# Four pairs of the second feed-forward as block products, with weight sums made ahead of it

## The chip, the cores and the metric

The kernel runs on one core of one Trainium2 chip. The metric is the device time of one execution in microseconds, the median of several runs. One core has five engines that work side by side: TensorE (PE, matrix products), VectorE (DVE), ScalarE (ACT), GpSimd (POOL) and SyncE (SP), and 16 DMA engines that move data between the chip's memory (DRAM) and the core's. Each engine works off its own instructions in order; waits between engines go by semaphores.

## The reference

One residual block for 256 tokens of width 1024: a feed-forward, a mix of two attention-like branches, a memory read, and a second feed-forward.

```python
def swiglu(h, w_in, w_down):
    gate, up = jnp.split(h @ w_in, 2, axis=-1)
    return (jax.nn.silu(gate) * up) @ w_down
...
        h = rmsnorm(x, ffn1_pre_g[l])
        x = x + 0.5 * rmsnorm(swiglu(h, ffn1_w_in[l], ffn1_w_down[l]), ffn1_post_g[l])

        h = rmsnorm(x, mix_pre_g[l])
        q_a, f_a, i_a, g_a, q_b, k_b, v_b, f_b, gates = jnp.split(h @ w_in[l], IN_OFFSETS, axis=-1)
        ...   # HGRN2 recurrence -> y_a, forgetting attention -> y_b, gated sum y
        x = x + rmsnorm(y @ w_out[l], mix_post_g[l])

        h = rmsnorm(x, mem_pre_g[l])
        mem_n = rmsnorm(mem, mem_kv_g[l])
        x = x + rmsnorm(mem_cross_attention(h, mem_n, w_mq[l], w_mkv[l], w_mo[l]), mem_post_g[l])

        h = rmsnorm(x, ffn2_pre_g[l])
        x = x + 0.5 * rmsnorm(swiglu(h, ffn2_w_in[l], ffn2_w_down[l]), ffn2_post_g[l])
```

The width of the feed-forward's inside (D_FF) is 2816. All inputs and outputs are float32.

## The kernel before

**Products.** Every operand is kept as two float32r parts, hi (rounded) and lo (the rest), and each product is made as three: hi·hi, hi·lo, lo·hi. Weights come as units of 128x1024 float32 (512 KB). `load_split` loads a unit on SP's queue into one of four `raw` buffers; ACT copies it to `hi` (L129), VectorE subtracts to make `lo` (L130); hi and lo have eight buffers each. The order of the units is that in which the code calls for them, and they are loaded and split that far ahead as the buffers allow. TensorE's order is the order in which its instructions are written, save for blocks that `after(i)` puts behind the i-th matmul of the log.

**Stages in time.** First feed-forward (to about 188 us of the span), the mix (projections i_a, f_a, q_a, g_a; HGRN2; q_b, k_b, v_b and the forgetting attention; gates; br_a, br_b; w_out), the memory read (mk, mv, mq, mo), the second feed-forward (from about 601 us), and a tail: the last norm, done by `post_last`, and the output.

**A feed-forward** goes over NFF = 11 chunks of 256 columns of gate and 256 of up. A plain chunk takes four units: for each half of the tokens (128), 8 blocks of 128 rows x 3 products of 512 columns go into a bank of PSUM; `act_evac` makes silu(gate)·up from it, `flush` turns that on TensorE (L386) and splits it, and `down` multiplies it with two units of the down weights, 24 products of 512 columns per chunk, into four accumulators that stay open over all chunks.

**Pairs as block products.** For a pair of chunks (c, c+1) named in QUADS_1 or QUADS_2, `quad` treats two token halves, two halves of the inner dimension and the two chunks as a 2x2 block product and makes it with seven products in place of eight (a scheme of Strassen's kind): 7 x 4 blocks x 3 = 84 products of 512 columns. It needs sums of activations (made once by `mixed`, with the splits and the row scale in it; this is `mix[0]`, the activations N) and sums of weight blocks. The sums of weights are made inside of `quad`: four units are loaded plain (to `raw`), four to two `wide` buffers, VectorE adds them (L446 to L449, and L503 in place), and `two` splits the sums as if they were loaded. `fourth_product` and `third_product` end the quad. In the last quad of a feed-forward that ends with it (`last`, c = 9) their order is the other way round. Both feed-forwards have quads at chunks 5 and 8, so that chunks 0 to 4, 7 and 10 are plain.

**The tail's warm-up.** In the second feed-forward, when the second half of chunk 10 has been evacuated, `act_evac` issues one Sqrt on a single column (L408); `post_last` needs a Sqrt at its end (L348).

**GpSimd** does little: the moves of the attention's cumulated logarithms through DRAM (`cd`, `cbc`, `cbm`, L885 to L935) with DMAs on its own queue, and two selects (L937).

The `wide` buffers hold the first heads, the weights of a quad, and in the mix the gates' bias rows (`brow`).

Of the kernel before, what the change touches and what calls it, by code (L numbers as in the profile page):

```python
# [49 lines left out]

QUADS_1 = (5, 8)
QUADS_2 = (5, 8)
# [18 lines left out]
def block_kernel(ctx: ExitStack, tc: tile.TileContext, wts, head_in, gf_in, x_in, mem_in, memT_in, cols, rows, fbias, masks, out):  # L71
# [194 lines left out]
    def mixed(X, r):  # L266

        row = row_of(r)
# [102 lines left out]
    def ffn(w_in, w_dn, X, r2, n_tok, i_row, quads, first_half, second_half=None):  # L371
# [46 lines left out]
        def quad(c, n_down):  # L418
# [10 lines left out]
            B11, B21, wide, first, second_, fourth = ([] for _ in range(6))  # L429
            for q in range(2):  # L430
                W = wp.tile([P, 2, 2, 512], F32, tag="wide", name=nm("wide"), bufs=2)
                raws = []
                for i in range(2):
                    u = _AT[w_in] + 4 * c + 2 * q + i
                    raw = wp.tile([P, D], F32, tag="raw", name=nm("raw"), bufs=4)
                    loads.append(nc.sync.dma_start(raw, wts[u - 4]).ins)
                    loads.append(nc.sync.dma_start(W[:, i].rearrange("p j n -> p (j n)"), wts[u]).ins)
                    hi, lo = parts_of()
                    split(hi, lo, raw)
                    B11.append((hi[:, :512], lo[:, :512]))  # L440
                    B21.append((hi[:, 512:], lo[:, 512:]))
                    raws.append(raw)
                wide.append(W)
                t1, t2, t4 = (m4([P, 2, 512], n="sum") for _ in range(3))
                for i in range(2):
                    V.tensor_tensor(out=t1[:, i], in0=raws[i][:, :512], in1=W[:, i, 0], op=ALU.add)  # L446
                V.tensor_tensor(out=t2, in0=t1, in1=W[:, :, 1], op=ALU.add)
                for i in range(2):
                    summed = V.tensor_tensor(out=t4[:, i], in0=t2[:, i], in1=raws[i][:, 512:], op=ALU.add).ins  # L449
                first.append(t1)  # L450
                second_.append(t2)
                fourth.append(t4)
            T1 = two(first[0]) + two(first[1])
# [29 lines left out]
            if len(late) == 2:  # L483
                flush(n + 4)
                flush(n + L_ACT)
            else:
                with tc.issue_after(summed):
                    flush(n + L_ACT)
# [5 lines left out]
            T2 = two(second_[0]) + two(second_[1])  # L494
            prods(b1, F(s2h, s2l), T2, False)
# [5 lines left out]
            T3 = []  # L501
            for W in wide:
                V.tensor_tensor(out=W[:, :, 0], in0=W[:, :, 0], in1=W[:, :, 1], op=ALU.add)  # L503
                T3 += two(W[:, :, 0])
# [7 lines left out]
            def fourth_product():  # L512
                T4 = two(fourth[0]) + two(fourth[1])
                prods(b1, X(1, 1), T4, False, True)
                act_evac(b1, c, 1)

            def third_product():
                B22 = two(wide[0][:, :, 1]) + two(wide[1][:, :, 1])
                prods(b2, F(s4h, s4l), B22, False, True)
                V.tensor_tensor(out=w, in0=b2, in1=w, op=ALU.subtract)  # L520
                act_evac(w, c + 1, 0)

            if last:
                down(n_down + 1, 1)
                flush_half(c + 1, 1, n + L_ACT)
                third_product()
                n = len(log)
                fourth_product()
                flush_half(c + 1, 0, n + 12)
            else:  # L530
                fourth_product()
                down(n_down + 1, 1)
                third_product()
# [47 lines left out]
        for c in range(n_tok, NFF):  # L581
# [6 lines left out]
            acts[c] = m4([P, 2, 2, T], F32R, "act")  # L588
            if c == 2 and first_half:
# [105 lines left out]

    ffn("f1_in", "f1_dn", X1, norm_1, 0, 0, QUADS_1, first)


    iv = [m4([P, 2, 512], n="iv") for _ in range(2)]
    for h in range(2):  # L700
# [5 lines left out]
        if h == 0:  # L706
            half(X2, r2, 1, G_MIX, m + L_IA)
    row2 = row_of(r2)
# [19 lines left out]
    for c in range(2):  # L728
# [12 lines left out]
        kT_.append(k)  # L741
    for c in range(2):
# [9 lines left out]
        qT_.append(q)  # L752

# [135 lines left out]
    for c in range(2):  # L889
        for name, lst, sc in (("k_b", kb_, 1.0), ("q_b", qb_, 1.0 / math.sqrt(128.0))):  # L890
# [7 lines left out]
            lst.append(t)  # L898
            if c == 0 and name == "k_b":
# [109 lines left out]
    for c in range(2):  # L1009
# [6 lines left out]
        vb_.append(t)  # L1016
    for h in range(2):
# [5 lines left out]
    brows = []  # L1023

    def gates(c):
        u = chunk("gates", c)
        z = m4([P, 2, 512], n="zg")
        if c % 2 == 0:
            brows.append(wp.tile([P, 2, D], F32, tag="wide", name=nm("brow"), bufs=2))
        brow = brows[-1][:, c % 2, :512]  # L1030
# [6 lines left out]
        zs.append(z)  # L1037

    m = len(log)
    gates(0)  # L1040
    for g in range(2):
# [20 lines left out]
    for c in (0, 2, 1, 3):  # L1062
        S.activation(zs[c], zs[c], AF.Sigmoid)
    g2 = load_row(1)
# [11 lines left out]
    for c in range(2):  # L1076
        for name, X, zc in (("br_a", OA, c), ("br_b", OB, 2 + c)):
            u = chunk(name, c)
            for h in range(2):
# [9 lines left out]
                if zc != c:  # L1089
                    za = zs[c][:, h]  # L1090
                    V.tensor_tensor(out=za, in0=za, in1=z, op=ALU.add)

# [13 lines left out]
    for h in range(2):  # L1106
        rows_proj(po[h], Y, "w_out", h, range(0, 4))
        if h == 0:
            y_T(1, 1, m + L_Y)
    rowm = row_of(rm)  # L1110
# [9 lines left out]
    for c in range(2):  # L1120
        u = chunk("mk", c)
        KM.more()
        for j in range(2):
# [4 lines left out]
            split(KM.h[c][:, js], KM.l[c][:, js], t)  # L1128
            if j == 0:
                half(X3, r3, c, G_MEM, m + (L_WO, L_MK)[c], m + (L_WO, L_MK)[c] + 16)  # L1130
    for c in range(2):
        u = chunk("mq", c)
        QM.more()
        for j in range(2):
            js = slice(2 * j, 2 * j + 2)
            ps = proj_col2(X3, u, (2 * j, 2 * j + 1))
            split(QM.h[c][:, js], QM.l[c][:, js], ps)

# [55 lines left out]

    m = len(log)
    mem_v(1)
    for i in range(2):
# [22 lines left out]
    ffn("f2_in", "f2_dn", X4, r4, 2, 3, QUADS_2, None, second)  # L1220
# [85 lines left out]
```

## Time and profile before

| | |
|---|---|
| median of 3 runs | 790.78 us (790.71 to 791.66) |
| the profiled execution's own time | 791.19 us |
| its span | 789.3 us |
| granted TensorE clock, mean | 0.999 |
| PE / DVE / ACT / POOL busy | 779.5 / 609.5 / 451.5 / 9.3 us |
| moved by DMA | 147.44 MB, mean 187 GB/s |

The span runs from the first instruction's start to the last end in the profile; the execution's own time has about 1.9 us around it. Busy time counts the work of an engine without its waits. TensorE's ends are modelled, so what counts for it is the time from start to start.

### The profile page before, as it was taken

How to read it: one execution, taken by the hardware profiler on the slowest of the kernel's cores; microseconds unless marked ns; L12 is line 12 of the kernel's file. 1: busy time of each engine (PE TensorE's matmuls, PEld its weight loads, DVE VectorE, ACT ScalarE, POOL GpSimd, SP SyncE). 2: the span in 40 equal slices, each digit the busy share in tenths (PEclk: the TensorE clock that was granted, in tenths of full speed). 3: DMA queues.
4: the chain of work that ended last, by engine and by line, in shares of the span. 5: the costliest groups of instructions: out<-in, count | busy, mean ns of one | idle time of the engine just before them, and what ended most of it. 6: DMA issues, size and time to landing. Idle time of an engine off the chain costs nothing.

```text
span 789.3 us, 12909 instructions
## 1 busy us (share of the span) xinstructions
PE 779.5 (99%) x5028; PEld 674.5 (85%) x5028; DVE 609.5 (77%) x944; ACT 451.5 (57%) x682; POOL 9.3 (1%) x21
## 2 busy tenths in 40 slices
PE   9999999999999999999999999999999999999996
PEld 7878888888899999998888888999888888888885
DVE  6798989978766898578685665965758799978963
ACT  7655665656853447348584444754636665664751
POOL 0000000000000100100000000000000000000000
PEclk9999999999999999999999999999999999999999
DMA  9766483384544555644497655456454545471441
GB/s 340 244 246 228 157 298 136 135 285 161 169 153 143 181 188 164 232 156 137 150 327 272 220 171 176 162 170 203 151 170 133 194 153 209 152 275 71 147 161 53
DMA packets 43692, 147.44 MB, mean 187 GB/s; under 512 B 4840, under 2 KB 8304, under 8 KB 43632
## 3 DMA queue, kind: packets, MB, share of 16 engines
q1 hardware_dynamic: 43024, 144.92, 53.7%
q0 software_dynamic: 464, 1.58, 0.6%
q8 instruction: 39, 0.64, 0.3%
q14 instruction: 21, 0.17, 0.1%
q10 hardware_dynamic: 144, 0.13, 0.0%
HBM read 145.56 MB, written 1.06 MB: 186 GB/s over the span
## 4 chain that ended last, share of the span: by engine, by line
PE 95%; DMA 2%; ACT 1%; DVE 1%; issue 0%; DVEq 0%; SPq 0%; ACTq 0%
PE mm L85 64%; PE acc L85 27%; PE tr L85 3%; DMA raw<-in_wts_dram 1%; PE tr L386 1%; PE tr L306 1%; DMA head<-in_head_dram 1%; ACT hi L129 0%; DVE lo L130 0%; PE tr L983 0%; PE tr L1072 0%; PE tr L1175 0%; ACT hT L148 0%; DVEq L1302 0%; SPq L655 0%
## 5 line engine op out<-in xcount | busy, mean ns | idle before, releaser
L130 DVE TENSOR_TENSOR lo<-raw,hi 128x1024 fp32r<-128x1024 f32 (+1 forms) x228 | 271.6, 1207 | 68.4 <-ACT hi L129 64.1
L129 ACT CAST hi<-raw 128x1024 fp32r<-128x1024 f32 (+1 forms) x228 | 232.2, 1036 | 127.0 <-PE mm L85 76.7
L85 PE MATMUL mm<-hi,hT 128*128 128x512 f32 (+1 forms) x496 | 189.7, 385 | 0.9 <-ACT hT L148 0.9
L85 PE MATMUL mm<-lo,hT 128*128 128x512 f32 (+1 forms) x496 | 190.2, 386 | 0.0
L85 PE MATMUL mm<-hi,lT 128*128 128x512 f32 (+1 forms) x496 | 188.5, 385 | 0.0
L85 PE MATMUL acc<-hi,act 128*128 128x512 f32 x352 | 113.2, 391 | 0.0
L85 PEld LDWEIGHTS mm<-hi,hT 128*128 128x128 f32 x496 | 93.1, 188 | 19.5 <-ACT hT L148 1.6
L85 PE MATMUL mm<-hT,hi 128*128 128x256 f32 x384 | 109.0, 284 | 0.1
L85 PE MATMUL mm<-hT,lo 128*128 128x256 f32 x384 | 109.0, 284 | 0.0
L85 PE MATMUL mm<-lT,hi 128*128 128x256 f32 x384 | 108.9, 284 | 0.0
L85 PEld LDWEIGHTS mm<-hi,lT 128*128 128x128 f32 x496 | 93.1, 188 | 17.7 <-DVE lT L264 0.7
L85 PEld LDWEIGHTS mm<-lo,hT 128*128 128x128 f32 x496 | 93.0, 188 | 16.5
L85 PEld LDWEIGHTS acc<-hi,act 128*128 128x128 f32 x352 | 66.0, 188 | 14.0 <-DVE act L149 0.5
L85 PEld LDWEIGHTS mm<-hT,hi 128*128 128x128 f32 x384 | 73.6, 192 | 0.4 <-issue 0.3
L85 PEld LDWEIGHTS mm<-lT,hi 128*128 128x128 f32 x384 | 73.6, 192 | 0.1
L85 PEld LDWEIGHTS mm<-hT,lo 128*128 128x128 f32 x384 | 73.6, 192 | 0.1
L85 PE MATMUL acc<-lo,act 128*128 128x512 f32 x176 | 69.2, 393 | 0.0
L85 PEld LDWEIGHTS acc<-lo,act 128*128 128x128 f32 x176 | 33.1, 188 | 6.6
L85 PE MATMUL acc<-hi,hT 128*128 128x512 f32 x96 | 35.6, 399 | 0.7 <-ACT hT L263 0.6
L148 ACT CAST hi<-sum 128x1024 fp32r<-128x1024 f32 x24 | 24.6, 1051 | 19.1 <-DVE sum L446 15.1
L85 PE MATMUL acc<-hi,lT 128*128 128x512 f32 x96 | 35.1, 393 | 0.0
L85 PE MATMUL acc<-lo,hT 128*128 128x512 f32 x96 | 34.9, 391 | 0.0
(233 smaller groups left out, 978.5 us busy)
## 6 DMA issues: line engine op xcount, KB each, us to landing
raw<-in_wts_dram SPq DMA_DIRECT2D x232, 512.0 KB, 4.4
wide<-in_wts_dram SPq DMA_DIRECT2D x16, 512.0 KB, 5.6
raw<-in_gf_dram SPq DMA_DIRECT2D x12, 344.0 KB, 3.8
head<-in_head_dram SPq DMA_DIRECT2D x8, 388.0 KB, 6.4
grow<-in_rows_dram SPq DMA_DIRECT2D x4, 512.0 KB, 6.2
xs<-in_x_dram SPq DMA_DIRECT2D x2, 512.0 KB, 8.6
cbm<-cd POOLq DMA_DIRECT2D x2, 512.0 KB, 9.3
brow<-in_rows_dram SPq DMA_DIRECT2D x4, 256.0 KB, 5.2
```

The costliest lines, as they stand in the source:

```text
L85: log.append(PE.matmul(*args, **kw).ins)
L129: S.copy(h, r)
L130: V.tensor_tensor(out=l, in0=r, in1=h.bitcast(F32), op=ALU.subtract)
L148: S.copy(hi, src)
L306: PE.transpose(ps[:, j * P : (j + 1) * P], src(kb), ident)
L386: PE.transpose(trv[:, j, h * P : (h + 1) * P], ats[c, h][:, j * P : (j + 1) * P], ident)
```

## The change

Four places change.

1. The second feed-forward has quads at 3, 5, 7 and 9, back to back to its end; only chunks 0, 1 and 2 are plain. The first keeps 5 and 8. The chain of `mixed` for the second is written into its chunk 2 (`L_MX` = 30 matmuls back); in the first it is issued where it was, but the chunks use its result one chunk later than before.
2. The weight sums of these four quads are no longer made in `quad`. Between the feed-forwards, 16 steps (4 quads x 2 x 2) make them: POOL's queue loads two units into a `wide` buffer, VectorE makes four adds of 128x512 in place (t1, t3, t2, t4), POOL's queue stores the result into DRAM tiles `sums[c]`, 64 DMAs of 512 KB in all (32 loads, 32 stores), and the load of the step after next follows (`load_step`, two `wide` buffers). The places of the steps are listed in SUMS_AT; seven loads come before the gates, where one `wide` buffer holds the bias rows, the others after.
3. In a quad with `sums`, each sum is loaded on SP's queue into `wide` (1 MB for each of the four sums) and split; the fourth plain block (`lower`) is loaded as two half-width pairs into `raw`. VectorE adds no weights in it. A quad's loads are 18 units of 512 KB, the four of its down weights with it.
4. In every quad `third_product` now comes ahead of `fourth_product`, and both downs ahead of them.

The warm-up Sqrt stays where it was in the code of `act_evac`: on the event that the second of the two halves of chunk 10 is evacuated. With a quad at 9, chunk 10 is finished within `third_product`, and `fourth_product` evacuates the second half of chunk 9 after it.

In numbers of instructions: 4492 matmuls of 4516 in the program order remain.

```diff
-QUADS_2 = (5, 8)
+QUADS_2 = (3, 5, 7, 9)
+L_MX = 30
+
+SUMS_AT = (
+    ("i_a", 0), ("f_a", 0), ("f_a", 1), ("q_a", 0), ("q_a", 1), ("q_b", 0), ("q_b", 1), ("gates", 2),
+    ("br_a", 0), ("br_b", 0), ("br_a", 1), ("br_b", 1), ("mk", 2), ("mk", 3), ("mq", 0), ("mq", 1),
+)
+TO_GATES = 7
...
-    def mixed(X, r):
-
-        row = row_of(r)
+    def mixed(X, r, back=0):
+
+        with after(len(log) - 1 - back):
+            row = row_of(r)
...
+            if sums:
+                for i in range(4):
+                    hi, lo = load_split(wts[_AT[w_in] + 4 * c + i - 4])
                     B11.append((hi[:, :512], lo[:, :512]))
                     B21.append((hi[:, 512:], lo[:, 512:]))
...
+                def sum_of(k):
+                    W = wp.tile([P, 2, D], F32, tag="wide", name=nm("wide"), bufs=2)
+                    for q in range(2):
+                        loads.append(nc.sync.dma_start(W[:, q], sums[c][(0, 3, 2, 1)[k], q]).ins)
+                    return two(W[:, 0].rearrange("p (i n) -> p i n", i=2)) + two(W[:, 1].rearrange("p (i n) -> p i n", i=2))
+
+                def lower():
+                    out = []
+                    for q in range(2):
+                        u = _AT[w_in] + 4 * c + 2 * q
+                        raw = wp.tile([P, D], F32, tag="raw", name=nm("raw"), bufs=4).rearrange("p (i n) -> p i n", i=2)
+                        loads.append(nc.sync.dma_start(raw, wts[u : u + 2, :, 512:].rearrange("i p n -> p i n")).ins)
+                        out += two(raw)
+                    return out
...
+            down(n_down + 1, 1)
             if last:
-                down(n_down + 1, 1)
                 flush_half(c + 1, 1, n + L_ACT)
-                third_product()
-                n = len(log)
-                fourth_product()
+            third_product()
+            n = len(log)
+            fourth_product()
+            if last:
                 flush_half(c + 1, 0, n + 12)
-            else:
-                fourth_product()
-                down(n_down + 1, 1)
-                third_product()
...
+            if quads and c == quads[0] - 1 and c == 2:
+                ready = mixed(X, r2, L_MX)
...
-            if quads and c == max(2, quads[0] - 3):
-                mix.append(mixed(X, r2))
-                X = mix[0][0]
-            if grow is None and c >= 4:
+            if quads and c == quads[0] - 3:
+                ready = mixed(X, r2)
+            if quads and c == max(2, quads[0] - 2):
+                mix.append(ready)
+                X = ready[0]
+            if grow is None and c >= quads[0] - 1:
                 grow = load_row(i_row)
...
+    sums = {c: dp.tile([4, 2, P, D], F32, name=f"sums_{c}") for c in QUADS_2}
+    steps = [(c, q, i) for c in QUADS_2 for q in range(2) for i in range(2)]
+    slots = []
+    brows = []
+
+    def load_step():
+        if len(slots) < len(steps) and (brows or len(slots) < TO_GATES):
+            c, q, i = steps[len(slots)]
+            W = wp.tile([P, 2, 2, 512], F32, tag="wide", name=nm("wide"), bufs=2)
+            for e in range(2):
+                G.dma_start(W[:, e].rearrange("p j n -> p (j n)"), wts[_AT["f2_in"] + 4 * (c + e - 1) + 2 * q + i])
+            slots.append(W)
+
+    def at(name, c=0):
+
+        if (name, c) not in SUMS_AT:
+            return
+        k = SUMS_AT.index((name, c))
+        (u, q, i), W = steps[k], slots[k]
+        last = next(x for x in reversed(nc.cur_bb.bb.instructions) if x.engine == mybir.EngineType.DVE)
+        t1, t4, t3, t2 = (W[:, a, b] for a in range(2) for b in range(2))
+        with tc.issue_after(last):
+            V.tensor_tensor(out=t1, in0=t1, in1=t3, op=ALU.add)
+            V.tensor_tensor(out=t3, in0=t3, in1=t2, op=ALU.add)
+            V.tensor_tensor(out=t2, in0=t1, in1=t2, op=ALU.add)
+            V.tensor_tensor(out=t4, in0=t2, in1=t4, op=ALU.add)
+        for e in range(2):
+            G.dma_start(sums[u][2 * e : 2 * e + 2, q, :, i * 512 : i * 512 + 512].rearrange("k p n -> p k n"), W[:, e])
+        load_step()
+
+    for _ in range(2):
+        load_step()
...
         zs.append(z)
+        at("gates", c)
...
-    ffn("f2_in", "f2_dn", X4, r4, 2, 3, QUADS_2, None, second)
+    ffn("f2_in", "f2_dn", X4, r4, 2, 3, QUADS_2, sums, None, second)
```

Calls of `at(name, c)` stand at the end of each of the pieces that SUMS_AT names, and `load_step` is called twice more around the gates.

More of the change, by code (lines that the diff above doesn't have):

```diff
@@ L368, in post_last, with ffn @@
             queue.dma_start(out[h * P : (h + 1) * P, a:b], xh)
-    def ffn(w_in, w_dn, X, r2, n_tok, i_row, quads, first_half, second_half=None):
+    def ffn(w_in, w_dn, X, r2, n_tok, i_row, quads, sums, first_half, second_half=None):
         acts = {}
@@ L427, in two @@
                 return [(hi[:, i], lo[:, i]) for i in range(2)]
[L429 to L439, printed above, removed]
+            B11, B21 = [], []
@@ L447, in quad @@
[L447 to L453, printed above, removed]
+                def sum_of(k):
[3 more added lines that the diff above has]
+                    return two(W[:, 0].rearrange("p (i n) -> p i n", i=2)) + two(W[:, 1].rearrange("p (i n) -> p i n", i=2))
@@ L485, in quad @@
                 flush(n + L_ACT)
+            elif sums:
+                flush(n + L_ACT)
             else:
@@ L500, in quad @@
                 flush_half(c, 0, n)
[L501 to L504, printed above, removed]
+            T3 = sum_of(2)
             prods(b1, F(s3h, s3l), T3, False)
@@ L1016, in block_kernel @@
         vb_.append(t)
+        at("v_b", c)
     for h in range(2):
```

72 lines of the change are left out of this document (56 added, 16 removed).

## The prediction

> **What bounds the kernel now.** I read the page first: busy time, and the chain that ended last.
>
> ```profile
> span 789.3 us, 12909 instructions
> PE 779.5 (99%) x5028; PEld 674.5 (85%) x5028; DVE 609.5 (77%) x944; ACT 451.5 (57%) x682; POOL 9.3 (1%) x21
> PE 95%; DMA 2%; ACT 1%; DVE 1%; issue 0%; DVEq 0%; SPq 0%; ACTq 0%
> ```
>
> TensorE works for 99% of the span and carries 95% of the chain, so whatever it no longer issues is gained, as long as nothing starves it. VectorE has 180 us free over the whole, and POOL nearly all. The waits view of TensorE is the second view, and names three waits:
>
> ```profile
> PE tr L85 <- DVE ones L198: 1.1, 1, 1.1
> PE mm L85 <- ACT hT L148: 0.9, 1, 0.9
> PE acc L85 <- ACT hT L263: 0.6, 1, 0.6
> ```
>
> Third, the chain, for what one product costs:
>
> ```profile
> 681.35 2.76 PE mm L85 x12
> 684.11 2.72 PE acc L85 x12
> ```
>
> Twelve 512-column products take 2.72 us from start to start: 0.227 us each. Fourth, windows, which tell where VectorE and the DMA have room. Columns are window, length, then busy us of PE, PEld, DVE, ACT and POOL, the granted clock, the DMA share and GB/s.
>
> ```profile
> 212.00:601.00 389.00, 388.79 (x3259) 353.11 (x3258) 280.22 (x470) 211.73 (x341) 7.26 (x12) 1.00 0.55 184
> 258.00:287.00 29.00, 28.92 (x659) 27.67 (x658) 26.70 (x46) 13.31 (x18) 2.27 (x6) 1.00 0.60 196
> 394.00:438.00 44.00, 44.00 (x196) 36.44 (x195) 30.41 (x51) 27.89 (x38) 0.00 (x0) 1.00 0.85 292
> 601.00:659.00 58.00, 58.00 (x270) 47.56 (x269) 50.59 (x91) 37.36 (x60) 0.00 (x0) 1.00 0.54 179
> 718.00:731.00 13.00, 13.00 (x61) 10.74 (x60) 12.82 (x17) 6.16 (x9) 0.00 (x0) 1.00 0.34 124
> 10.00:20.00 10.00, 10.00 (x46) 8.26 (x45) 9.19 (x13) 8.83 (x15) 0.00 (x0) 1.00 1.03 408
> ```
>
> The first row is the stretch in which the sums are to be made; VectorE has 109 us free there. The clock is 1.00 throughout.
>
> **TensorE's share of the change.** A plain pair of chunks has 96 input products (two chunks, two halves, 8 blocks, 3 products each), a pair as block products 84 (7 x 4 x 3). Two more pairs save 24 products, the down projections stay: 24 x 0.227 = **-5.4 us**, all on the path.
>
> In the first feed-forward the mixed activations, still made at the same place, are used one chunk later. The 0.9 us wait above (on hT L148) is for them, in the chain at
>
> ```profile
> 45.23 1.05 ACT hi L129
> 46.28 0.95 ACT hT L148
> ```
>
> The chunk that takes its place uses plain activations that have long been there. **-0.8 us**: next late are that chunk's own splits, which the weight loads still pace. In return third and fourth product change places in all quads but the last, so the flush after the quads loses a cover; I allow **+0.4**, most of one eviction (0.59 in the first row of the tail below).
>
> **VectorE.** These groups give its prices (busy us, then mean ns):
>
> ```profile
> L130 DVE TENSOR_TENSOR lo<-raw,hi 128x1024 fp32r<-128x1024 f32 x216 | 261.3, 1226 | 64.8 <-ACT hi L129 60.7
> L446 DVE TENSOR_TENSOR sum<-raw,wide 128x512 f32<-128x512 f32 x16 | 10.6, 686 | 0.8 <-DMA raw<-in_wts_dram 0.8
> L447 DVE TENSOR_TENSOR sum<-sum,wide 128x1024 f32<-128x1024 f32 x8 | 9.8, 1222 | 0.1
> L503 DVE TENSOR_TENSOR wide<-wide 128x1024 f32<-128x1024 f32 x8 | 9.7, 1221 | 0.0
> ```
>
> A quad takes 84 + 48 products x 0.227 = 30.0 us of TensorE. Its VectorE work now: 18 splits (14 of inputs, 4 of down weights) x 1.23 = 22.1, sums 4 x 0.69 + 2 x 1.22 + 4 x 0.69 + 2 x 1.22 = 10.4, evictions some 5: 37 us, and so VectorE is full in the window 718 to 731. The new quad has 27 us against 30. VectorE thus stops being the tight engine in the second feed-forward, which bought nothing before since TensorE did not wait there.
>
> Added are 64 adds of 128x512: 64 x 0.69 = 44 us, in 16 groups of four (2.7 us) between about 205 and 545 us. They fit into 109 us on the whole. Between VectorE and TensorE stand eight buffers of split units, each good for 12 products or 2.72 us, so up to 22 us of lead; with a third of that, 7 us, a group hides unless it falls into a chain that TensorE is waiting for. One does: step 6 comes after q_b's second chunk, at
>
> ```profile
> 342.29 1.22 DVE L130 TENSOR_TENSOR lo<-raw,hi 128x1024 fp32r<-128x1024 f32 x1
> 343.50 0.21 DVE L215 TENSOR_SCALAR v<-ss 128x1 f32<-128x1 f32 x1
> 346.22 1.41 DVE L927 SCALAR_TENSOR_TENSOR G<-acc,rstd,G 128x512 f32<-128x512 f32 x2
> 347.67 0.34 DVE L968 SCALAR_TENSOR_TENSOR p<-tr,ct,cbm 128x128 f32<-128x128 f32 x1
> ```
>
> VectorE has no gap here: the norm runs from 343.50 to the eviction at 346.22 that frees an accumulator for the products of v_b. A group of 2.7 us lies in that chain; bounds 0 and 2.7, and since the order of TensorE puts v_b's other products in front, I take the middle, **+1.2**. A second tight place is the HGRN start (258 to 287, VectorE 92% full): bounds 0 and 2.7, near 0 as units are ahead, **+0.2**. Were all 16 groups exposed, 16 x 2.4 (start to start) = 38 us.
>
> Making the mixed activations of the second feed-forward moves from behind its third chunk into it. Five kinds of VectorE operations of 1.22 us, two each, some 12 us, now compete with the splits of that chunk in a window with 7.4 us free of 58. Bounds 0 and 2.5 (two splits late); I take **+0.4**.
>
> **The queues and the DMA.** POOL gets 32 loads and 32 stores of 512 KB, 33.5 MB more between 190 and 550. Only two wide buffers serve, so a step's load waits on the stores of the step two earlier. What two such transfers take stands in POOL's timeline, for cbm and its selects:
>
> ```profile
> 317.96 1.07 POOL L935 DMA_DIRECT2D cbm<-cd  x2 [13.54 <-PE acc L85]
> 326.37 1.09 POOL L937 TENSOR_SCALAR_AFFINE_SELECT cbm<-cbm 128x1024 f32<-128x1024 f32 x1 [7.34 <-DMA cbm<-cd]
> 328.84 1.21 POOL L937 TENSOR_SCALAR_AFFINE_SELECT cbm<-cbm 128x1024 f32<-128x1024 f32 x1 [1.38 <-DMA cbm<-cd]
> ```
>
> 8.4 us to the first and under 10.9 to the second: stores and loads take 17 to 21 us. In most steps 22 us or more are there. The shortest is from step 12 to step 14:
>
> ```profile
> 516.53 0.69 DVE L149 TENSOR_TENSOR lT<-km,hT 128x512 fp32r<-128x512 f32 x1 [0.31 <-ACT hT L148]
> 533.28 0.69 DVE L149 TENSOR_TENSOR lT<-mm,hT 128x512 fp32r<-128x512 f32 x1
> 537.40 0.69 DVE L149 TENSOR_TENSOR lT<-mm,hT 128x512 fp32r<-128x512 f32 x1 [2.31 <-ACT hT L148]
> 541.38 3.50 DVE L130 TENSOR_TENSOR lo<-raw,hi 128x1024 fp32r<-128x1024 f32 x3 [3.29 <-ACT hi L129]
> ```
>
> From 517.2 to 534.0 are 16.8 us, 14.4 of them behind the adds. Step 14 is then 3 to 6 us late, and VectorE, which works in order, holds back the splits and evictions queued behind it. Its idle time there is 2.31 + 3.29 = 5.6 us: covered, narrowly. Also queued on POOL are the mask's loads and selects, now behind the stores of step 5; the selects were done at 330, and their reader (p<-tr,ct,cbm) starts at 347.67. I take **+0.3** for all this.
>
> [...]
>
> In the quads the loads become the heavy part: 18 units x 0.524 MB = 9.4 MB in 30 us, 315 GB/s. The trace moved 408 from 10 to 20 us, and 292 at a share of 0.85, so it can; nothing added.
>
> **The tail.** The last rows of ACT, and VectorE's reciprocal behind them:
>
> ```profile
> 765.17 0.59 ACT L148 CAST act<-tr 128x512 fp32r<-128x512 f32 x1 [1.82 <-PE tr L386]
> 766.07 1.28 ACT L408 ACT_TABLE_LOAD   x1
> 783.08 0.29 ACT L348 ACTIVATE y<-ss,v 128x1 f32<-128x1 f32 x1
> 783.75 0.16 DVE L355 RECIPROCAL y<-y 128x1 f32<-128x1 f32 x1
> ```
>
> A warm-up square root after the last Silu loads its table early, so the square root at 783.08 needs none. In the changed kernel's instruction order the warm-up stands behind the first half of chunk 9, and another Silu (its second half) follows. Silu's table comes back, and the last square root has to load its own, 1.28 us, in the open. The reciprocal also waits for other work till 783.75, so 1.28 - 0.38 = **+0.9**.
>
> **Sum**, against the profiled execution (span 789.3, 791.2 with what lies around it): -5.4 - 0.8 + 0.4 + 1.2 + 0.2 + 0.4 + 0.3 + 0.9 = -2.8, so 788.4. The median of the runs, 790.78, is 0.4 lower: **788.0 us**.
>
> **Rivals.** (A) *VectorE blocked behind POOL's transfers; slower.* If a pair of transfers takes 12 us rather than 8 to 10, beside the weight stream, step 14 is 24 - 14.4 = 9.6 late, 4 beyond its cover, and steps 13 and 15, with about 20 us, 4 more; with 1 or 2 at the HGRN steps, 788 + 9 = 797. It decides from about 10 us a pair on. For it: in 394 to 438 the DMA share is 0.85 already. [...] 0.16.
>
> (B) *The quads are bound by DMA; slower.* Some 4.2 MB are ahead in buffers (eight units), so four quads need (37.7 - 4.2) MB in 122 us, 275 GB/s. At 240 they take 140 us: +18, 806. From about 260 on down it is slower than before. For it: means of 124 to 292 in the windows; against: those are demand, and 408 was had. 0.06.
>
> (C) *Given back; no change.* The adds cost their full 2.7 in three chains (step 6, HGRN, the mixed activations) instead of 1.8 in all, so 788.0 + 8.1 - 1.8 = 794 at worst, at half of that surplus 791. 0.16.
>
> (D) *Nothing starves.* Only products, first wait and tail count: 790.8 - 5.4 - 0.8 + 0.9 = 785.5; without the tail's load 784.6. 0.20.
>
> **How the numbers follow.** Forecast 788.0 with 0.42. Its bounds: all unknown costs at nothing 785.5, the chains full 791. The range of 784.6 to 795 leaves out most of B, the upper part of A. What a measurement can tell from no change is 0.2%, 1.6 us: faster is below 789.2, slower above 792.4. Faster: D, four fifths of the forecast (0.34) and a little of C (0.08): 0.62. Slower: A, B and a little of C: 0.23. Same: 0.15.
>
> **What the changed profile would show.** PE 24 products fewer, its busy time 5 us less; no wait on hT L148 at 46 us; waits of TensorE at 346 to 350 on VectorE's G, of about a microsecond; VectorE's adds without idle time on DMA except at step 14; second-feed-forward windows at DMA shares near 0.8 with VectorE about 90% busy; a table load before the last square root. I am wrong if the waits view shows weights (hi, lo) missing in the quads (B), or idle of VectorE on wide of several us that reaches TensorE (A).

## The result: slower, 801.1 us against 790.9

| | before | changed |
|---|---|---|
| median | 790.89 us (790.71 to 791.66, 4 runs) | 801.1 us (800.04 to 802.45, 4 runs) |
| ratio | | 1.0128, interval 1.0111 to 1.0146 |
| span of the profiled execution | 789.3 us | 800.6 us |

The forecast was 788.0, range 784.6 to 795. The page of the changed kernel, first its parts 1, 3 and 4:

```profile
span 800.6 us, 13165 instructions
...
PE 778.9 (97%) x5004; PEld 671.3 (84%) x5004; DVE 646.0 (81%) x1004; ACT 470.2 (59%) x704; POOL 50.1 (6%) x85
...
q0 software_dynamic: 9680, 35.14, 11.9%
...
PE 77%; DMA 9%; DVE 8%; ACT 3%; issue 2%; POOL 0%; DVEq 0%; ACTq 0%; POOLq 0%; SPq 0%
```

TensorE issues 24 matmuls fewer (5004 for 5028), as meant; the counts 4492 and 4516 of the program order stand in no profile, only their difference does. But 23% of the chain now runs through other engines, where it was 5%. TensorE's waits view says where at once; the same view of before had nothing over 1.1 us:

```profile
PE tr L1264 <- DVE pm L1260: 9.0, 1, 9.0
PE acc L94 <- DVE lo L139: 1.3, 1, 1.3
...
PE acc L94 <- ACT act L157: 0.6, 1, 0.6
```

One wait of 9.0 us, in the memory read: the transposes of the softmax (L1264, which was L1175) come late. Four landmarks of the chain, in the changed kernel and then in the kernel before, tell what each stretch lost (start, length, what):

```profile
396.32 53.97 PE mm L94 x238
...
575.64 1.94 PE tr L1264 x8
...
594.53 18.65 PE acc L94 x82
...
616.20 10.28 PE mm L94 x45
```

```profile
393.20 53.97 PE mm L85 x238
...
563.27 0.87 PE tr L1175 x8
...
579.40 18.65 PE acc L85 x82
...
601.09 10.23 PE mm L85 x45
```

At 393 the changed kernel is 3.1 us late; at the transposes 12.4; at mo's products 15.1, and the same at the start of the second feed-forward. So the wait cost 9.3, and the stretch right behind it 2.7 more. The windows show by what (window, length, busy us of PE, PEld, DVE, ACT, POOL, clock, DMA share, GB/s):

```profile
566.00:576.00 10.00, 1.00 (x5) 0.58 (x4) 7.53 (x15) 6.15 (x12) 0.00 (x0) 0.75 1.02 379
576.00:582.00 6.00, 6.00 (x21) 5.00 (x20) 2.92 (x5) 3.95 (x11) 0.00 (x0) 0.57 0.19 79
...
693.00:724.00 31.00, 31.00 (x141) 25.44 (x140) 25.41 (x28) 21.77 (x27) 0.00 (x0) 1.00 0.89 311
```

After the pause the granted clock is 0.57 for 6 us. The last row holds a quad: it runs as forecast, TensorE never idle, VectorE 82% busy, 311 GB/s. From 616 to the end of the last product the changed kernel makes good 4.8 us.

**Where the 9 us come from.** SP's timeline, then POOL's, then the waits of SP's queue, then VectorE's waits for the loads of steps (us in all, times, longest):

```profile
526.02 17.24 SPq L137 DMA_DIRECT2D raw<-in_wts_dram  x7
554.81 0.33 SPq L450 DMA_DIRECT2D wide<-sums  x1
555.25 1.85 SPq L137 DMA_DIRECT2D raw<-in_wts_dram  x4
```

```profile
532.49 1.11 POOL L754 DMA_DIRECT2D wide<-in_wts_dram  x2 [6.58 <-DMA sums<-wide]
533.59 1.47 POOL L771 DMA_DIRECT2D sums<-wide  x2
546.35 1.11 POOL L754 DMA_DIRECT2D wide<-in_wts_dram  x2 [11.29 <-DMA sums<-wide]
547.73 1.46 POOL L771 DMA_DIRECT2D sums<-wide  x2 [0.26 <-issue]
```

```profile
SPq L450 <- DMA sums<-wide: 11.3, 1, 11.3
```

```profile
DVE wide L766 <- DMA wide<-in_wts_dram: 6.1, 2, 4.0
```

SP issues nothing from 543.3 to 554.8. It stands at L450, the first load of finished sums for the quad at 3. The first of these sums is split at 657.6, and the stores of that quad's four steps were issued by 254; what is missing is a *wide buffer*, which step 14 holds until its stores have landed. Step 14's stores stand on POOL behind the load of step 15, and that behind step 13's stores (11.3 us). Behind L450 on SP stand the weights of mo. They land from 560 on; VectorE, in order, waits for them ahead of the softmax's maxima; the transposes wait for these. The chain that ended last goes that way:

```profile
556.19 9.71 DMA raw<-in_wts_dram
...
569.62 1.13 DVE lo L139
570.76 0.68 DVE mx L1254 x2
...
574.27 1.24 DVE pm L1260
```

TensorE had run out of work at 566.6. VectorE's own waits for the steps' loads (the row at L766) are 4.0 us at step 14 and 2.1 at step 15.

### The profile page after: what moved, and what is told of

It reads as the page before. It is cut to its first block, busy times and chain, and to the rows that moved or that the text cites. A ratio compares the mean times of both kernels' runs of the same rounds, so it can differ in the third digit from the quotient of the medians.

```text
span 800.6 us, 13165 instructions
## 1 busy us (share of the span) xinstructions
PE 778.9 (97%) x5004; PEld 671.3 (84%) x5004; DVE 646.0 (81%) x1004; ACT 470.2 (59%) x704; POOL 50.1 (6%) x85
## 4 chain that ended last, share of the span: by engine, by line
PE 77%; DMA 9%; DVE 8%; ACT 3%; issue 2%; POOL 0%; DVEq 0%; ACTq 0%; POOLq 0%; SPq 0%
PE mm L94 47%; PE acc L94 24%; DMA raw<-in_wts_dram 5%; PE tr L94 3%; DVE lo L139 3%; DMA sums<-wide 2%; ACT hi L138 2%; PE tr L396 1%; PE tr L316 1%; DMA wide<-in_wts_dram 1%; DMA head<-in_head_dram 0%; ACT hT L157 0%; DVE lT L158 0%; PE tr L1264 0%; ACT junk L244 0%
## 5 line engine op out<-in xcount | busy, mean ns | idle before, releaser
L139 DVE TENSOR_TENSOR lo<-raw,hi 128x1024 fp32r<-128x1024 f32 (+1 forms) x228 | 271.0, 1202 | 65.8 <-ACT hi L138 61.6
L94 PE MATMUL mm<-hi,hT 128*128 128x512 f32 (+1 forms) x448 | 171.7, 387 | 0.5 <-DVE G L944 0.4
L94 PE MATMUL mm<-lo,hT 128*128 128x512 f32 (+1 forms) x448 | 171.8, 387 | 0.0
L94 PE MATMUL mm<-hi,lT 128*128 128x512 f32 (+1 forms) x448 | 171.4, 387 | 0.0
L94 PE MATMUL acc<-hi,act 128*128 128x512 f32 x352 | 113.2, 391 | 0.7 <-ACT act L157 0.6
L94 PE MATMUL mm<-hT,hi 128*128 128x256 f32 x384 | 109.0, 284 | 0.6 <-DVE zf L946 0.6
L94 PE MATMUL mm<-hT,lo 128*128 128x256 f32 x384 | 109.0, 284 | 0.0
L94 PE MATMUL mm<-lT,hi 128*128 128x256 f32 x384 | 108.9, 284 | 0.0
L94 PEld LDWEIGHTS mm<-hi,hT 128*128 128x128 f32 x448 | 84.7, 189 | 17.2 <-ACT hT L272 0.7
L94 PEld LDWEIGHTS mm<-hi,lT 128*128 128x128 f32 x448 | 84.5, 189 | 15.9 <-DVE lT L273 0.5
L94 PEld LDWEIGHTS mm<-lo,hT 128*128 128x128 f32 x448 | 84.4, 189 | 14.7
L94 PEld LDWEIGHTS acc<-hi,act 128*128 128x128 f32 x352 | 66.0, 188 | 15.3 <-ACT act L157 1.2
L94 PEld LDWEIGHTS mm<-hT,hi 128*128 128x128 f32 x384 | 73.6, 192 | 0.9 <-ACT hi L138 0.8
L94 PEld LDWEIGHTS mm<-lT,hi 128*128 128x128 f32 x384 | 73.6, 192 | 0.2
L94 PEld LDWEIGHTS mm<-hT,lo 128*128 128x128 f32 x384 | 73.6, 192 | 0.1
L94 PE MATMUL acc<-lo,act 128*128 128x512 f32 x176 | 69.2, 393 | 1.3 <-DVE lo L139 1.3
L158 DVE TENSOR_TENSOR lo<-wide,hi 128x1024 fp32r<-128x1024 f32 x40 | 47.7, 1220 | 3.5 <-ACT hi L157 2.9
L157 ACT CAST hi<-wide 128x1024 fp32r<-128x1024 f32 x40 | 41.8, 1053 | 12.2 <-DVE wide L494 3.4
L94 PEld LDWEIGHTS acc<-lo,act 128*128 128x128 f32 x176 | 33.1, 188 | 8.3 <-DVE lo L139 1.8
L771 POOL DMA_DIRECT2D sums<-wide x32 | 23.5, 734 | 243.7 <-DVE wide L768 222.3
L94 PE MATMUL mm<-hi,sh 128*128 128x512 f32 x96 | 37.5, 390 | 0.0
```

The costliest lines, as they stand in the source:

```text
L94: log.append(PE.matmul(*args, **kw).ins)
L139: V.tensor_tensor(out=l, in0=r, in1=h.bitcast(F32), op=ALU.subtract)
L157: S.copy(hi, src)
L158: V.tensor_tensor(out=lo, in0=src, in1=hi.bitcast(F32), op=ALU.subtract)
L771: G.dma_start(sums[u][2 * e : 2 * e + 2, q, :, i * 512 : i * 512 + 512].rearrange("k p n -> p k n"), W[:, e])
```

## The experiments

All kernels below start from the changed kernel; where one has edits of earlier ones too, the text says so. Times are medians; ratios are against the kernel before, run beside them.

**Is it the queue?** The loads of sums are ordered behind mo's on SP.

```diff
+        entry = loads[-1]          # on entry of ffn: mo's last load
...
+                        with tc.issue_after(entry):
                             loads.append(nc.sync.dma_start(W[:, q], sums[c][(0, 3, 2, 1)[k], q]).ins)
```

> The changed kernel with one thing different: on SP's queue the first two loads of sums of the second feed-forward stand behind the loads of mo's weights, not among them. Three theories of the 9.0 us in which TensorE waits for pm (566 to 576 us) in the changed kernel, with the half clock that follows some 12 us. Queue: SP stands from 543.3 to 554.8 at a load of sums whose wide buffer is not free before step 14's stores have landed, and mo's units stand behind it; the wait goes, and the run takes 789 us (801.1 - 12). VectorE: its adds of steps 14 and 15 wait 4.0 and 2.1 us for their loads and hold up what is behind; these waits stay, and so do 6 us or more of TensorE's: 795 or above. Bandwidth: the DMA share is 1.02 from 566 to 576 and the units come late for want of it; some of the wait stays, 793 to 800.

Measured 794.25 us (790.51 to 798.42), ratio 1.0034 (1.0009 to 1.0059); the profiled execution 791.92. TensorE's wait and VectorE's own waits for the adds:

```profile
PE tr L1266 <- DVE pm L1262: 1.1, 1, 1.1
```

```profile
DVE wide L768 <- DMA wide<-in_wts_dram: 4.1, 2, 2.3
```

The wait fell from 9.0 to 1.1, with VectorE's late loads still at 4.1 (6.1 in the changed kernel) and the DMA as full (share 1.00 from 548 to 566, 0.88 in the changed kernel). The queue theory holds for most of the wait: the profiled execution is 10.5 us faster than that of the changed kernel. But the median fell by 6.9 only, is 5 above what that theory forecast and lies where the bandwidth theory had it (793 to 800), and the runs now lie 8 us apart. What is left of the wait in this profile has a late weight in its chain:

```profile
547.20 9.74 DMA raw<-in_wts_dram
```

In that stretch the longest load of a weight took 5.3 us before the change. So the queue is not all of it. Which waits the longer executions have is not shown.

**The two ends.** The first feed-forward as before the change; the warm-up Sqrt behind the last cast.

```diff
-            if quads and c == max(2, quads[0] - 2):
+            if quads and c == (2 if sums else quads[0] - 3):
...
+            if not sums:
+                fourth_product()
+                down(n_down + 1, 1)
+                third_product()
+                return
...
+            cast = flush_half(NFF - 2, 1, m + L_Y)
+            with tc.issue_after(cast):
+                S.activation(warm, ones[:, 0:1], AF.Sqrt)
```

> The changed kernel with two places put back or mended, both far from the mix. In the first feed-forward the mixed activations are used at once again, and third and fourth product are in the old order: TensorE's waits of 1.3 (57.6 us) and 0.6 us (170 us) go and the old one of 0.9 (45.8 us) is back; the first feed-forward ends 1.0 us earlier, as before the change (products of L94 after 188.5 and not 189.5). In the tail the square root that warms the table stands behind the last cast: the load of the table of 1.28 us before the last square root goes, and the stretch from the end of the last junk to the end of the span is 6.2 again and not 7.2. Together -1.9: 799.2. If the first feed-forward's loss is not of the two edits but of something else, only the tail's 0.9 goes.

Measured 804.23 us (800.73 to 805.86), ratio 1.0153, where 799.2 was forecast. The tail did as expected. In the changed kernel, then in this one:

```profile
793.20 0.19 ACT L244 ACTIVATION_READ_ACCUMULATOR junk<-acc 128x1 f32 x1
793.41 1.28 ACT L358 ACT_TABLE_LOAD   x1
794.71 0.29 ACT L358 ACTIVATE y<-ss,v 128x1 f32<-128x1 f32 x1
```

```profile
794.70 0.19 ACT L245 ACTIVATION_READ_ACCUMULATOR junk<-acc 128x1 f32 x1
794.93 0.29 ACT L359 ACTIVATE y<-ss,v 128x1 f32<-128x1 f32 x1
```

The wait of 1.3 us at 58 us is gone too. But the end of the first feed-forward got worse with the old order of products, so its loss is not of that order alone. (In two later kernels with the first loads held back, one with each order, TensorE is busy for 19.79 and 19.71 us from 160 to 180.) Here the windows before the change, in the changed kernel and in this one:

```profile
150.00:160.00 10.00, 10.00 (x45) 8.26 (x45) 9.28 (x11) 6.03 (x9) 0.31 (x1) 1.00 0.52 171
...
170.00:180.00 10.00, 10.00 (x48) 8.04 (x47) 4.66 (x6) 3.56 (x7) 0.00 (x0) 1.00 0.59 200
```

```profile
150.00:160.00 10.00, 10.00 (x46) 8.28 (x45) 8.47 (x10) 4.88 (x8) 1.24 (x3) 1.00 0.98 371
...
170.00:180.00 10.00, 9.26 (x42) 7.06 (x41) 5.34 (x7) 3.75 (x7) 0.00 (x0) 1.00 0.66 216
```

```profile
170.00:180.00 10.00, 7.20 (x25) 5.25 (x24) 4.99 (x6) 4.03 (x7) 0.00 (x0) 0.83 0.81 262
```

From 150 to 160 the DMA share is 0.98, where it was 0.52: POOL's first four loads start at 149, long before their adds at 204, because only their buffers hold them. In this kernel's chain a weight unit loaded at 155 takes 9.0 us to land.

**Earlier steps, and no adds at all.**

```diff
-... ("q_b", 1), ("gates", 2), ... ("mk", 2), ("mk", 3), ("mq", 0), ("mq", 1),
+... ("q_b", 1), ("v_b", 0), ("v_b", 1), ("gates", 2), ... ("mk", 2), ("mk", 3),
-TO_GATES = 7
+TO_GATES = 9
```

> The changed kernel with two steps moved: after v_b's two chunks in place of mq's two, nine loads ahead of the gates, so that the last sums are made at mk (about 523 us) and not at 555. SP's loads of the sums come behind mo's by this too. Queue and VectorE theories both let the 12 us go: 789 or so. Against the first run of this set it tells what two more groups of adds cost in the attention (342 to 394 us, VectorE 44 of 53 us busy before): by the prediction's price up to 2.7 us each, 789 to 793.

Steps at v_b's two chunks in place of mq's: 800.83 us (796.19 to 803.07), ratio 1.0105. The wait for pm is gone here too, but the attention's own chain pays: waits of 2.0 and 1.5 us around 380 to 400, behind weights that took 6.9 and 7.4 us to land. Well over the price I had forecast.

Then the adds left out:

```diff
-        with tc.issue_after(last):
-            V.tensor_tensor(out=t1, in0=t1, in1=t3, op=ALU.add)
-            ...
```

> The changed kernel without the 64 adds: every load and store stays, so the sums are unsummed weights. What is lost in the HGRN stretch (258 to 300 us: 1.6 us more lost by TensorE than before the change) is gone if VectorE's adds made it, and stays if the transfers did. The stores no longer wait for adds, POOL runs ahead, and the wait at 566 goes by every theory: 788.

820.99 us, ratio 1.037 (1.0322 to 1.0418): 33 us off the forecast. Without adds the stores follow their loads at once, and POOL runs through the steps as fast as the DMA lets it. From 160 to 180 TensorE was busy for 14.36 us of 20 at 412 GB/s (DMA share 1.02). In the gates the first experiment's cause shows by itself, on a VectorE that has no adds to make (SP's timeline, and TensorE's waits):

```profile
434.58 0.70 SPq L329 DMA_DIRECT2D grow<-in_rows_dram  x1
464.76 0.33 SPq L450 DMA_DIRECT2D wide<-sums  x1
```

```profile
PE mm L94 <- DVE zg L1168: 18.5, 1, 18.5
```

SP stood 29.5 us at a load of sums with weights behind it, until POOL's last stores had landed. Whether the adds made the loss in the HGRN stretch this run can't tell: POOL's transfers had left that stretch (170 GB/s from 258 to 300, 277 in the changed kernel).

**Holding the first loads back.**

```diff
+    gate = s1(name="gate")
+    ready = G.tensor_tensor(out=gate, in0=r2[0], in1=r2[0], op=ALU.add).ins
+    with tc.issue_after(ready):
         for _ in range(2):
             load_step()
```

> The kernel with sums loads behind mo's, and one thing more: POOL's first four loads (steps 0 and 1) are held back by a one-column add on POOL that reads the mix's first scale, ready at about 186 us; they start there and not at 149. If these 2 MB, in the stretch where the DMA share was 0.52 and is now 0.98 (150 to 160 us), are what delays the last units of the first feed-forward, TensorE's waits at 170 us go and 160 to 180 loses 0.3 us and not 1.4 to 1.9: 1.5 us off, and less spread between runs. If the loss there is of the new order of third and fourth product, it stays.

The loads of sums stay behind mo's. 796.2 us (791.17 to 796.67), ratio 1.0058. The four loads start at 196, and the loss at 170 to 180 is nearly gone:

```profile
170.00:180.00 10.00, 9.79 (x48) 7.80 (x46) 5.13 (x7) 3.55 (x7) 0.00 (x0) 1.00 0.63 209
```

The time did not fall, nor did the spread: this execution waits 2.6 us for pm again, beside 8.8 us of VectorE's waits for late loads of the steps. The chain into that wait goes through a step's load that took 7.95 us to land and VectorE's work behind it, so this part of the wait is VectorE's, as rival A had it.

Then the tail's edit on top of it:

> The held-back one with the tail's warm-up behind the last cast: 0.95 us less than the held-back one, 1.28 of table load less 0.4 that VectorE needs anyway. 788.5 by the profile; against before -2 if the waits of TensorE in the mix stay at what the first run of this study had.

790.93 us (788.9 to 796.85, 12 runs), ratio 1.0016 (0.9999 to 1.0033). Its best execution comes within 0.4 of the forecast of 788.5, the median is 2.4 above it. That it is 5.3 below the kernel without this edit is more than the 0.95 of the tail: executions of the same program differ by as much. The profiled one, 795.26, waits 4.2 us for pm with VectorE standing 9.6 us at late loads; the chain there goes through two weight units that took 9.5 and 10.4 us to land. In this one, late weights and late loads of the steps are not told apart.

And other places for the steps besides (the tail's edit stays):

```diff
-... ("q_a", 0), ("q_a", 1), ... ("br_b", 1), ("mk", 2), ("mk", 3), ("mq", 0), ("mq", 1),
+... ("br_b", 1), ("w_out", 0), ("mk", 0), ("mk", 3), ("mq", 0), ("mq", 1), ("mv", 1),
-TO_GATES = 7
+TO_GATES = 5
```

> As the held-back one, with the tail's warm-up behind the last cast (-0.95) and the steps laid out anew: none at q_a's two chunks nor at q_b's place after them changed, one each after w_out's first half, mk's first and mv's second in their place (mk's third falls away). The HGRN stretch (258 to 300 us) then loses 3.3 us, as before the change, not 5.2 to 5.4, if the adds at q_a made the difference: -2.0. A price for the new places, at most 2.7 each where a chain is tight (w_out, mk). Forecast 787 against 791 for the held-back one's quiet runs; 793 if the new places are tight.

795.58 us (791.81 to 797.34), ratio 1.0053. The tight places moved: waits of 3.9 and 2.0 us at 507 to 515, where a weight took 9.5 us to land and VectorE waited 5.3 us for a step's load.

**What precomputed sums are worth.**

```diff
-    ffn("f2_in", "f2_dn", X4, r4, 2, 3, QUADS_2, sums, None, second)
+    ffn("f2_in", "f2_dn", X4, r4, 2, 3, QUADS_2, None, None, second)
```

> The changed kernel with four quads at 3, 5, 7, 9 in the second feed-forward, but their sums made inside of them as before, nothing in the mix. By the prediction's count VectorE needs 37 us a quad against TensorE's 30: some 7 us of waits in each of four, less what is split ahead of the first and what the tail absorbs, so 785.4 + 15 to 28 = 800 to 813, with VectorE full in the quads. If VectorE keeps up (its splits overlap to 1.13 us each, 35 us), 795.

802.75 us, ratio 1.0155, as forecast. Two of four quads:

```profile
671.00:703.00 32.00, 28.86 (x128) 22.67 (x127) 31.25 (x37) 18.54 (x24) 0.00 (x0) 1.00 0.48 165
...
735.00:767.00 32.00, 28.01 (x125) 21.95 (x124) 31.49 (x38) 18.47 (x25) 0.00 (x0) 1.00 0.59 197
```

VectorE is 98% busy, TensorE idles 3 to 4 us a quad. The reason for making the sums ahead was sound: with sums inside, four quads do not pay.

**All places mended, steps spread:**

```diff
-        entry = loads[-1]          # on entry of ffn
+        entry = loads[-1]          # ahead of chunk 2's loads
...
+    ("i_a", 0), ("f_a", 0), ("f_a", 1), ("q_a", 0), ("q_b", 0), ("q_b", 1), ("gates", 2), ("br_a", 0),
+    ("br_b", 0), ("br_a", 1), ("br_b", 1), ("mk", 2), ("mq", 0), ("mv", 0), ("mo", 0), ("mo", 1),
+TO_GATES = 6
```

> All mended places together: first loads held back, the first quad's sums loaded behind the second feed-forward's first chunks, the warm-up behind the last cast, and the steps spread so that no load has to come within 14 us: one step fewer at the HGRN start (q_a's second chunk), mk and mq with one each, and the last three at mv and mo (about 555, 575 and 585 us). What was left of the wait for pm (1.1 to 4.4 us in the runs before, beside VectorE's waits of 4 to 10 us for late loads of steps 14 and 15) goes if the late loads made it: no wait over 1 us behind 300 us, and 786.5, faster than before by 4. If it is the DMA's load in that stretch as such, 1 to 3 us of it stay: 788 to 790.

791.63 us (787.24 to 794.36, 12 runs), ratio 1.0007 (0.999 to 1.0024). The profiled execution is its fastest, 787.24 with a span of 785.5, and waits nowhere over 1.1 us. So the layout can give 3.5 us, but most executions do not: the median lies above both forecasts.

With the first feed-forward's two edits undone, as in the second run:

> The same with the first feed-forward as before the change (mixed activations used at once, fourth product ahead of third). Its loss from 40 to 180 us was 1.9 before the change, and 1.3 to 2.4 in the runs with held-back loads. If the new order of the first feed-forward gains what the prediction gave it (0.4), this is 0.4 slower than the other of this pair; if the waits for lo at 58 us are of the new order, it is up to 1 us faster.

791.64 us, ratio 1.0007: the first feed-forward's edits are not measurable here.

**Transfers or adds?** Both kernels are the spread kernel with a part left out, so that neither makes the sums. One keeps all adds, on a resident buffer, and loads original weights in the quads; the other keeps all transfers and adds 8 columns of each 512.

```diff
-            W = wp.tile([P, 2, 2, 512], F32, tag="wide", name=nm("wide"), bufs=2)
-            for e in range(2):
-                G.dma_start(W[:, e]..., wts[...])
+            W = held                                  # loaded once
-        for e in range(2):
-            G.dma_start(sums[u]..., W[:, e])
```

> The spread kernel without POOL's 64 transfers: all adds stay, on one resident buffer, and the quads load original weights in place of the sums, as many bytes. Two theories of why the spread kernel ranges from 787.2 to 794.4 us. Transfers: 33.5 MB out of turn delay single weight units, or come late themselves and hold VectorE up; without them the runs lie within 2 us of each other, as before the change, and at 785.5 to 786.5. VectorE: the 44 us of adds use up the lead of the splits, so that every late unit is felt; then the spread stays and the median is 789 or more.

787.19 us (786.19 to 787.48), ratio 0.9952 (0.9939 to 0.9964).

```diff
-            V.tensor_tensor(out=t1, in0=t1, in1=t3, op=ALU.add)     # and three more
+            V.tensor_tensor(out=W[:, :, :, :8], in0=W[:, :, :, :8], in1=W[:, :, :, 8:16], op=ALU.add)
```

> The counterpart: the spread kernel with all of POOL's transfers, but in place of the four adds of 128x512 of each step one of 128x2x2x8, so that loads and stores are paced by VectorE as before and VectorE is spared 40 us. By the transfers' theory the spread stays (787 to 793, median 790); by VectorE's the runs draw together at 785.5 to 786.5.

787.55 us (786.61 to 788.72), ratio 0.9965 (0.9951 to 0.9979).

I had set the two up as rivals, each as the one cause, and as that both fell: without either the loss is gone and the runs draw together (1.3 and 2.1 us apart, 5 runs each), together they cost 4 us (791.63, 12 runs, from 787.2 to 794.4; the kernel before ranged from 789.4 to 795.0 beside them, so a part of that range need not be the change's). The transfers alone still make VectorE wait 5.2 us for late loads. Why each alone is harmless is argued, not shown: VectorE can take late loads with 40 us less to do, and without transfers fewer weights come late.

**The adds on GpSimd.**

```diff
+            V.tensor_tensor(out=mark, in0=ones[:, 0:1], in1=ones[:, 0:1], op=ALU.add)
+        seen = s1(name="seen")
+        turn = G.tensor_tensor(out=seen, in0=mark, in1=mark, op=ALU.add).ins
+        with tc.issue_after(turn):
-            V.tensor_tensor(out=t1, in0=t1, in1=t3, op=ALU.add)
+            G.tensor_tensor(out=t1, in0=t1, in1=t3, op=ALU.add)     # and three more
```

> The spread kernel with the 64 adds on GpSimd instead of VectorE; of each step VectorE makes one 128x1 operation that tells GpSimd its turn. If what costs is that VectorE works on the adds and stands at late loads, this is at 787.5 as the one with small adds, within 2 us. If adds on GpSimd hold VectorE up in another way (a group takes longer there, so that stores and loads come later, or the two engines get in each other's way), the wait is back at the quads or in the mix: 790 or more.

806.97 us, ratio 1.0213 (1.0195 to 1.0231), 15.3 above the spread kernel: the second case. One of POOL's four adds, then VectorE's splits:

```profile
L772 POOL TENSOR_TENSOR wide<-wide 128x512 f32<-128x512 f32 x16 | 22.6, 1411 | 0.0
```

```profile
L138 DVE TENSOR_TENSOR lo<-raw,hi 128x1024 fp32r<-128x1024 f32 x216 | 277.0, 1299 | 63.5 <-ACT hi L137 58.8 <-PE mm L93 1.8
```

By its line an add takes 1.41 to 1.69 us in the mean on GpSimd (0.69 on VectorE), and VectorE's splits take 1299 ns in the mean, 1221 in the spread kernel. Two splits in VectorE's timeline, then the adds in POOL's:

```profile
597.35 1.23 DVE L138 TENSOR_TENSOR lo<-raw,hi 128x1024 fp32r<-128x1024 f32 x1 [1.45 <-ACT hi L137]
600.07 2.32 DVE L138 TENSOR_TENSOR lo<-raw,hi 128x1024 fp32r<-128x1024 f32 x1 [1.49 <-ACT hi L137]
```

```profile
600.01 1.29 POOL L772 TENSOR_TENSOR wide<-wide 128x512 f32<-128x512 f32 x1
601.38 2.17 POOL L773 TENSOR_TENSOR wide<-wide 128x512 f32<-128x512 f32 x1
```

The split at 597.35, with no add on GpSimd, takes 1.23 us; that at 600.07, beside two adds, 2.32. So the splits get slower beside the adds; by what, no run shows. How much of the 15.3 us is of the slower splits and how much of the longer groups of adds is not told apart.

**Half the steps.** Quads at 5, 7 and 9, the first with sums inside, the others made ahead in eight steps; the spread kernel's other edits stay.

```diff
-QUADS_2 = (3, 5, 7, 9)
+QUADS_2 = (5, 7, 9)
...
+    ("i_a", 0), ("f_a", 1), ("q_b", 0), ("gates", 2), ("br_b", 0), ("br_b", 1), ("mk", 2), ("mq", 0),
+TO_GATES = 3
```

> Quads at 5, 7 and 9 in the second feed-forward: the first makes its sums inside, as both did before the change, the other two have theirs made in the mix in eight steps, half the adds and transfers. TensorE saves 12 products against before, 2.7 us. If eight steps are below the point where late loads are felt and the quad at 5 keeps up as before, 788.0 and a spread of 2 us; if the quad at 5 lacks VectorE's plain chunk behind it, its 37 us against 30 cost 2 to 4: 790 to 792.

788.91 us (788.17 to 789.96, 11 runs), ratio 0.9979 (0.997 to 0.9988): 0.2% faster than the kernel before, forecast 788.0. It saves only 12 products, but its executions lie within 1.8 us of each other, and TensorE's longest wait behind the start is 0.2 us:

```profile
PE mm L93 <- issue: 0.2, 1, 0.2
PE acc L93 <- ACT act L156: 0.2, 1, 0.2
```

## Why the prediction was wrong

**The step that failed is the queues.** The prediction priced them at +0.3 and said of SP's queue nothing at all. It followed POOL's and VectorE's and found step 14 late by 3 to 6 us and covered by VectorE's idle time. Step 14 was late by 4.0 us, and that was not what cost most. The late buffer was wanted by a third queue too: SP's, where the first load of sums stands ahead of mo's weights. Price in the profiled execution: 9.3 + 2.7 = 12.0 us of the 14.1 by which the span missed (-2.8 forecast, +11.3 measured). With that load behind mo's weights 10.5 us came back in the profile and 6.9 in the median, so the queue is the larger part, not the whole. The 2.7 are the halved clock after the pause, which was in no price.

**Rival A** had the right neighbourhood and the wrong queue; that its 797 came nearer than the forecast is in the main luck. Its premise, 24 us for a pair of stores and a pair of loads, did not hold: from the first store of step 12 to the add of step 14 it was 17.1 us (523.95 to 541.07), from the stores of step 13 to the add of step 15 18.7, within the 17 to 21 that the forecast used. POOL's longest wait for a pair of stores was the 11.3 of step 13; its 13 such waits sum to 82.2. The wait on VectorE that A describes was seen once with SP mended (2.6 us, first loads held back); in two other such profiles (1.1 and 4.2 us) the chain goes through late weights.

**Loads out of turn.** I costed the first feed-forward at -0.4. Its first wait, on hT, is gone, but one of 1.3 us came behind it (lo, L139), on the split of a down weight that VectorE made after the last splits of the mixed activations, so that the -0.8 became -0.2 (TensorE's products of 64.36 us start at 64.18). At its end (L94 after 189.5 for L85 after 188.5) it was +1.0. The four early loads were not thought of there, although the diff issues them ahead of the mix. The HGRN stretch cost 1.6 more where I had 0.2, measured by TensorE's starts from the transposes at 211.7 us to those at 292.0. By the same starts it is 0.3 more with the adds alone, 1.4 with the transfers alone, but 0.8 in the spread kernel that has both: this points to the transfers, on one profile each.

**Right within three quarters of a microsecond:** the tail (+0.9 forecast, 1.0 measured: the end comes 7.2 us behind the last read of the sums of squares, before 6.2), the quads (from 601 to that read -4.8, forecast -5.4 + 0.4), the DMA of the quads (311 GB/s without a wait, forecast 315; rival B fell), and step 6 (+0.5 from the HGRN stretch to 393, forecast 1.2). VectorE's load of the adds was counted right (16 x 4 of 0.69 us) but judged group by group: a group was to hide in a lead of 7 us, and nothing was set aside for a late unit that has used the lead already. That adds and transfers together cost 4 us that neither costs alone was the second error, in a layout without the first.

**Open:** what keeps the median of the first mended kernel 5 us above its forecast, and which wait the longer executions of the spread kernel (up to 794.4) have: the profiled one was its fastest. That waits move between pm, the HGRN stretch and mo is from single profiles of its relatives.

## What to carry to other kernels

A load that is moved or added has to be followed on its own queue with the buffer it goes to: ask who holds that buffer, on which queue *that* release stands, and what stands behind the load. Extra traffic needs a reason to start late as well as early: here POOL's queue, with nothing else to do, started it 55 us ahead of its use. When spare time of an engine and spare bandwidth are both spent, price them together, and look at the spread of the runs and not only at the median: the spread kernel's ranged over 7 us where its median was that of the kernel before.

## What the runs showed that I had not expected

After a pause of 9.0 us TensorE was granted half its clock for some 5.5 us (0.50 from 575.64 to 581.2): products started 0.43 us apart, not 0.227, 2.7 us in all (timeline). In the held-back kernel with the tail's edit, where the pause is 4.2 us, the granted clock is 0.81 in the mean from 558 to 576; in the spread kernel, without such a pause, 1.00.

```profile
578.23 0.63 PE L94 MATMUL mm<-hi,lT 128*128 128x512 f32 x1
578.65 0.63 PE L94 MATMUL mm<-hi,hT 128*128 128x512 f32 x1
...
581.68 0.39 PE L94 MATMUL mm<-hi,lT 128*128 128x512 f32 x1
581.91 0.39 PE L94 MATMUL mm<-hi,hT 128*128 128x512 f32 x1
```

The same program's executions lay 7 us apart (787.2 to 794.4) with the transfers on one queue and the weights on another, where without the transfers, or with small adds, they lay within 2.1 us (5 runs each).
